# Token sums in the q/k/v stage, gate rows in the last merge phase, weights' squares into free buffers, and B's spatial output in SBUF

## The chip, the core and the metric

The kernel runs on one core of one Trainium2 chip. The metric is the device time of one launch in microseconds (us): the kernel before takes 2449.18 us, the median of three runs. Of the core's engines, TensorE (PE in the profile, PEld for its weight loads) does the matmuls and transposes, VectorE (DVE), ScalarE (ACT) and GpSimd (POOL) the elementwise work, and SyncE (SP) issues most of the DMAs; ACT and POOL issue some.

## The reference

One layer of a mixer network for 2048 sample tokens and 128 prompt tokens (2176 in all, 17 tiles of 128), width 1024. The two groups share the weights and differ in the conditioning vector and in the states that they start from.

```python
shift, scale, gate = ada_mod(c, w_ada, b_ada)          # silu(c) @ w_ada + b_ada
xn = rmsnorm(x, ln_g) * (1 + scale) + shift
qkv, beta, dec, z_a, u_b, v_b, z_b, x_c, z_c, gates = split(xn @ w_in)
qkv = silu(conv3(qkv))                                 # q, k, v of 4 heads x 128
o_a = rmsnorm(gated_delta(q, k, v, g, beta) in both directions) * silu(z_a)   # A
o_b = u_b * (w_spatial @ rmsnorm(v_b) + b_spatial) * silu(z_b)                # B, blocks of 128 tokens
o_c = fft2(x_c).real * silu(z_c)                                              # C
merged = sum over n of sigmoid(gates[n]) * (o[n] @ w_branch[n])               # n = A, B, C
y = rmsnorm(x + gate * (merged @ w_out), final_g)
```

The outputs are y for both groups and the prompt's final states of the delta rule. Everything is float32. The kernel multiplies the large matrices in split form: a value is a float16 high part plus a float16 low part, and a product is three matmuls (high x high, high x low, low x high) into one PSUM bank.

## The kernel before

**Order of the stages.** The conditioning sums (shift and scale; the third part, gate, comes later); normalisation and transposes of x into two SBUF tiles, xh and xl (channels on partitions, 2176 tokens), with z_a's projection; q/k/v (12 column tiles of 128, five token blocks each, four of 512 and one of 128); B's v (17 token tiles); the SGU stage, B's u and z (four column tiles, five blocks); branch C with its Fourier transform; six merge phases; the output projection, whose result, gated and normalised, is stored.

**Who sets the order.** The program is written in one order, and a scheduler of the framework then fixes the order of the instructions on each engine, by priorities and a model of times; evictions written under high priority go first. Within an engine the order does not change on the chip. A class Pace (L244) runs one generator beside the main work: each `tick` adds the main work's estimated us, and for every quota (1.2 in q/k/v, 1.6 later) the generator advances by one yield. In q/k/v the generator is decays (L406): for each of 17 tiles, two broadcast loads of log decays from DRAM (gamR), eight DVE operations (L484), a yield, an exponential on ACT (L486), and a store. From the v stage on it is delta (L821): prep for each of 17 tiles (L540: load q, k, v rows, L548, transpose at L549, norms, products with the decays), base_inverse and level for the triangular solves (L598, L639), then scan_dir for the forward and the backward direction, 17 steps each (L739; its matmuls are `b<-sv,R`, `b<-u,skn`, `b<-S,sk` and, in attend, `b<-u,sqk`), and in the backward direction finish (L804) for each tile: sum of both directions, norm, gate, branch A's output to DRAM, and its square sum (L807 to L818).

**q/k/v (L490 to L516).** Each block's product is evicted by ACT into raw (L503); ps_mm has three PSUM banks. After five blocks the three taps of the conv run on DVE (L506 to L508), sigmoids on ACT (L511), products on POOL (L512), and the column tile goes to DRAM.

**v and SGU.** For each token tile the v stage evicts v, norms it, multiplies it by w_spatial, and writes the result vs to DRAM (L888, L889). The SGU stage reads the blocks of vs back into the ring st (L944), and multiplies u onto them (L948). gate_unit (L839) makes silu(z) and the product (L846 to L852). Beside it runs x_sums (L900): sums of quarters of xh, xl for the merge phases, which use a seven-product scheme for 2 x 2 blocks of tokens and channels (S1 to S4 by 80 POOL operations, L917 to L934, a cast on ACT, L912, and a subtraction on DVE, L913, for each of 32 pieces, and a DMA).

**Branch C** shares a ring, us, between the prompt's product yp (L1078) and later products; cf holds its constants.

**Merge.** The phases are (branch, token half): (1,0), (2,0), (1,1), (2,1), (0,1), (0,0), branch 0 being A. A phase has four items (two column tiles each). merge_item (L1162) computes the sigmoid gates from xh and xl in seven products, then the branch's products, and adds to accumulators mrow, which are kept in DRAM between phases. branch_half (L1126) scales and splits the branch's rows to float16 in side steps, one per unit of work. fetch_gate (L977) loads gate weights one item ahead: squares (L1001) for the scale, sums of quarters on POOL (L1011 to L1016), splits (L1008, L1009, L1020), and a write of the split weights for later phases. In phase 0 each item also makes two of eight gate rows (gate_row, L1283): 128 columns of w_ada, 16 DVE operations (ada_sum, L301 to L308) of 128 columns, two matmuls, a store in DRAM. In the last phase each item prepares two column tiles of w_out (out_w, L1322).

Of the kernel before, what the change touches and what calls it, by code (L numbers as in the profile page):

```python
# [110 lines left out]
def hybrid_flow_kernel(ctx: ExitStack, tc: tile.TileContext, x_prompt, x_sample, state_delta, c, c_ctx, ln_g, w_ada,  # L111
# [294 lines left out]
    def decays():  # L406
# [82 lines left out]

    pace.start(decays(), 1.2)  # L490
    for ct in range(12):
        w = getw(1, 2)
        for half in range(1):
            raw = sb(a1p, [P, LP], "raw")
            G.memset(raw[:, 0:1], 0.0)
            G.memset(raw[:, NS + 1:NS + 3], 0.0)
            G.memset(raw[:, LP - 1:LP], 0.0)
            for t0, tn in TBS:
                ps = bank(ps_mm, [P, tn])
                gemm_T(ps, w, 0, xh[:, :, t0:t0 + tn], xl[:, :, t0:t0 + tn])  # L500
                o = t0 + 1 if t0 < NS else t0 + 3
                with tc.high_priority():
                    A.activation(raw[:, o:o + tn], ps, AF.Copy, scale=w.inv)  # L503
# [27 lines left out]
    def chunk_off(t):  # L531
        return t * P if t < 16 else NS + 2
# [7 lines left out]
    def prep(g, ci, t):  # L540
        tok = sb(dq, [P, 2, WB], "tok")
        qr = sb(dq, [P, H, P], "qr")
        ss = sb(dq, [P, 2, H], "ss2", bufs=2)
        for part in range(3):
# [26 lines left out]
        dc = sb(dq, [P, 2, WB], "dc")  # L571
        SY.dma_start(dc, decD[t])
# [283 lines left out]
    vsD = dram("vs", [4, P, NTOK])  # L856
# [12 lines left out]
    vinv = sb(ep, [P, 4], "vinv", bufs=1)  # L869
    for i in range(4):  # L870
        V.tensor_copy(vinv[:, i:i + 1], vw[i].inv)
    for t in range(NCH):
# [6 lines left out]
        vs = sb(bp, [P, 4, P], "vs")  # L879
# [9 lines left out]
        SY.dma_start(vsD[:, :, t * P:(t + 1) * P].rearrange("g p t -> p g t"), vs)  # L889
# [3 lines left out]

    XSLOT = {"A11": (0, 0), "A12": (0, 1), "A22": (1, 1), "S1": (2, 0), "S2": (2, 1), "S3": (3, 0), "S4": (3, 1)}
    xqD = [{n_: dram(f"xq{h}{n_}", [P, 2, 4, 512], F16) for n_ in XSLOT} for h in range(2)]

    def quarter(t, b, kh):
        return t[:, 4 * kh:4 * kh + 4, 512 * b:512 * b + 512]

    def x_sums(sp):  # L900
        for hf in range(2):
            for n_, b, kh in (("A11", 0, 0), ("A12", 0, 1), ("A22", 1, 1)):
                for l, t in enumerate((xh, xl)):
                    SY.dma_start(xqD[hf][n_][:, l], quarter(t, 2 * hf + b, kh))
            yield 1
            for k in range(4):
                (a11, a12), (a21, a22) = [[[t[:, k + 4 * kh, 512 * b:512 * b + 512] for t in (xh, xl)] for kh in range(2)]
                                          for b in (2 * hf, 2 * hf + 1)]

                def put(n_, v):  # L910
                    o = sb(sp, [P, 2, 512], "xo", F16, bufs=3)
                    A.copy(o[:, 0, :], v)  # L912
                    V.tensor_tensor(o[:, 1, :], v, o[:, 0, :], ALU.subtract)  # L913
                    SY.dma_start(xqD[hf][n_][:, :, k, :], o)

                s1, s2, s3, tm = [sb(sp, [P, 512], n_) for n_ in ("s1", "s2", "s3", "tm")]
                G.tensor_tensor(s1, a21[0], a22[0], ALU.add)  # L917
                G.tensor_tensor(tm, a21[1], a22[1], ALU.add)
                G.tensor_tensor(s1, s1, tm, ALU.add)
                put("S1", s1)  # L920
                yield 1
                G.tensor_tensor(s2, s1, a11[0], ALU.subtract)
                G.tensor_tensor(s2, s2, a11[1], ALU.subtract)
                put("S2", s2)
                yield 1
                tm = sb(sp, [P, 512], "tm")
                G.tensor_tensor(s3, a11[0], a21[0], ALU.subtract)
                G.tensor_tensor(tm, a11[1], a21[1], ALU.subtract)
                G.tensor_tensor(s3, s3, tm, ALU.add)
                put("S3", s3)  # L930
                yield 1
                s4 = sb(sp, [P, 512], "s3")
                G.tensor_tensor(s4, a12[0], s2, ALU.subtract)
                G.tensor_tensor(s4, s4, a12[1], ALU.add)  # L934
                put("S4", s4)
                yield 1

    sps = ExitStack()
    xsums = x_sums(pool(sps, "sp", 1))
    for g in range(4):  # L940
        uw, zw = getw(2, 2)
        for ti, (t0, tn) in enumerate(TBS):
            st = sb(ep, [P, tn], "st", bufs=3)
            SY.dma_start(st, vsD[g][:, t0:t0 + tn])  # L944
# [5 lines left out]
            next(xsums, 0)  # L950
            gate_unit(1, g, ti, zw, st)
            next(xsums, 0)
    for _ in xsums:
        pass
    sps.close()
# [21 lines left out]
    def fetch_gate(i):  # L977
# [22 lines left out]
        for c in range(2):  # L1000
            A.activation(tiles[2 + c][:, :, 1], sts[c], AF.Square, accum_out=ss[:, c:c + 1])  # L1001
# [11 lines left out]
        split(tiles[2], sts[0])  # L1013
        split(tiles[0], tq)
        G.tensor_tensor(tq[:, 0], b21, tq[:, 0], ALU.subtract)
        G.tensor_tensor(tq[:, 1], b22, b12, ALU.subtract)  # L1016
        A.activation(tiles[3][:, 0, 0], b22, AF.Copy, scale=s)
# [3 lines left out]
        split(tiles[1], tq)  # L1021
        for z, t in enumerate(tiles):
            m = 1024 if z == 3 else 2048
            SY.dma_start(gwD[n][j][:, z, 0:m], flat(t)[:, 0:m])
# [30 lines left out]
    for g in range(4):  # L1055
        xw, zw = getw(2, 2)
        for gh in range(1):
            yT = sb(fp, [P, NTOK], "yT", bufs=1)
            Y1 = sb(fp, [P, 64, 32], "Y1")
            for q in range(0, NCH, 4):  # L1060
# [13 lines left out]
                else:  # L1074
                    ps = bank(ps_x, [P, 2 * P])
                    mm(ps, xc[:, 0, :], K["dftcs"])
                    yp = sb(fp, [P, 2 * P], "us", bufs=2)
                    V.tensor_copy(yp, ps)  # L1078
                    ps = bank(ps_x, [P, P])
                    mm(ps, K["dftcs"][:, 0:P], yp[:, 0:P], True, False)  # L1080
                    mm(ps, K["dftms"], yp[:, P:2 * P], False, True)
                    A.copy(yT[:, NS:NTOK], ps)
                pace.tick(1.5 * qn)
            yv = yT[:, 0:NS].rearrange("p (r k) -> p k r", k=64)
            for q4 in range(4):
# [14 lines left out]
                pace.tick(3.5)  # L1100
                us = sb(fp, [P, 8, 32], "us", bufs=2)
# [24 lines left out]
    def branch_half(n, hf, prompt):  # L1126
# [8 lines left out]
        def steps():  # L1135
            for b in range(2):
                for g in range(4):
                    st = sb(big, [P, 512], "mrow", bufs=6)
                    t0 = 1024 * hf + 512 * b
                    SY.dma_start(st, obD[n][g, :, t0:t0 + 512])  # L1140
# [21 lines left out]
    def merge_item(i, o16, side, swap, first):  # L1162
# [5 lines left out]

        def unit():
            pace.tick(2.8)  # L1170
            next(side, 0)

        mr = {}
        for r_, c in ((0, 0), (1, 1), (0, 1), (1, 0)):
            mr[r_, c] = sb(big, [P, 512], "mrow", bufs=6)
            if not first:
                t0 = 1024 * hf + 512 * r_
                SY.dma_start(mr[r_, c], mD[2 * j + c][:, t0:t0 + 512])
# [104 lines left out]
    def gate_row(blk):  # L1283
        st = sb(wp, [P, KT, P], "wst", bufs=2)
        SY.dma_start(st, w_ada_[:, 2 * D + blk * P:2 * D + (blk + 1) * P].rearrange("(k p) c -> p k c", p=P))
        ps = bank(ps_x, [2, P])
        acc = sb(ep, [P, 512], "st", bufs=3)[:, 0:2 * P].rearrange("p (g c) -> p g c", g=2)
        ada_sum(acc, st, range(KT))
        for g in range(2):
            mm(ps, sel[:, g, :], acc[:, g, :], g == 0, g == 1)  # L1290
        gr = sb(big, [2, P], "gr", bufs=1)
        br2 = sb(big, [2, P], "br2", bufs=1)
        SY.dma_start(br2, b_ada_[None, 2 * D + blk * P:2 * D + (blk + 1) * P].to_broadcast([2, P]))
        V.tensor_add(gr, ps, br2)
        SY.dma_start(gateD[:, blk * P:(blk + 1) * P], gr)

    def run_phase(p, each=None):
        n, hf = PH[p]
        o16, inv, side = branch_half(n, hf, PH[p] in FRESH)
        for j in range(4):  # L1300
# [3 lines left out]
            if each is not None:  # L1304
                each(2 * j)
                each(2 * j + 1)
# [3 lines left out]
    run_phase(0, gate_row)  # L1310
    for p in range(1, 4):
        run_phase(p)
# [47 lines left out]

    order = [16] + list(range(8, 16)) + list(range(8))
    run_phase(4)
    run_phase(5, out_w)
# [71 lines left out]
```

## Time and profile before

| | us |
|---|---|
| median of 3 runs | 2449.18 |
| lowest, highest | 2446.91, 2450.38 |
| profiled execution | 2451.27 |
| its span | 2449.5 |

A line of a table by windows gives the stretch in us from the span's start, its length, then for each engine its busy time and number of instructions, then PEclk, the mean clock granted to TensorE (1 is full), the share of time in which DMA engines were busy, and GB/s. A line of the waits gives the waiting engine, its operation and line, what it waited for, and then us in total, the number of times, and the longest. A line of the groups gives line, engine, operation, result and operands with shapes and count, then busy us and mean ns of one, then idle time in front of them with what ended it. A letter q behind an engine marks its queue.

### The profile page before, as it was taken

The page shows a single profiled execution, that of the slowest core. Times are in us where ns is not written, and L with a number is a line of the kernel's source. Part 1 is how long each engine was busy: PE and PEld are TensorE (multiplying, and loading weights), DVE is VectorE, ACT ScalarE, POOL GpSimd, SP SyncE. Part 2 cuts the span into 40 slices and gives each one's busy share as a digit, 9 for nine tenths or more (in the row PEclk, how much of TensorE's full clock was granted, in tenths as well). Part 3 has the DMA queues.
Part 4 walks back from the last instruction along what each step waited for, and adds up shares of the span by engine and source line. Part 5 has one row for each costly group of instructions (what it writes and reads, how often), then busy time and mean ns, then how long its engine had stood idle before and what let it go on. Part 6 is the DMA issues. An engine that isn't in the chain of part 4 may idle for free. (4 is left out here: it accounts for less than half of the span.)

```text
span 2449.5 us, 43951 instructions
## 1 busy us (share of the span) xinstructions
PE 2250.5 (92%) x16804; PEld 1374.8 (56%) x16804; DVE 1439.1 (59%) x3228; ACT 825.3 (34%) x1539; POOL 1026.2 (42%) x1216
## 2 busy tenths in 40 slices
PE   7998999998988898989978879989999999989998
PEld 3564444796444677768555555656665545534443
DVE  5636743467659486655776777766555345452554
ACT  3544533322433333222522224332223233331332
POOL 2411222344986333234553454765443334323453
PEclk9999999998998999999989889999999999989999
DMA  8615622475675756324764556769656556963542
GB/s 287 207 54 191 222 90 77 155 206 125 202 203 150 211 183 155 65 68 144 262 219 152 164 175 206 246 217 327 204 183 217 164 169 218 303 220 118 179 155 103
DMA packets 437436, 440.63 MB, mean 180 GB/s; under 512 B 94449, under 2 KB 333034, under 8 KB 435690
## 3 DMA queue, kind: packets, MB, share of 16 engines
q1 hardware_dynamic: 422282, 384.33, 51.3%
q0 software_dynamic: 10048, 40.13, 4.2%
q10 hardware_dynamic: 4896, 13.37, 1.5%
q8 instruction: 132, 2.16, 0.4%
q14 instruction: 78, 0.64, 0.1%
HBM read 269.35 MB, written 168.39 MB: 179 GB/s over the span
## 5 line engine op out<-in xcount | busy, mean ns | idle before, releaser
L160 PE MATMUL b<-xh,w 128*128 128x512 f16 (+1 forms) x3976 | 1045.3, 350 | 26.4 <-ACT raw L503 13.1
L160 PEld LDWEIGHTS <-w 128*128 128x128 f16 x5964 | 535.1, 99 | 575.6 <-issue 61.1
L160 PE MATMUL b<-xl,w 128*128 128x512 f16 (+1 forms) x1988 | 678.0, 350 | 0.5 <-POOL xl L382 0.4
L160 PE MATMUL b<-big,b 128*128 128x512 f16 (+1 forms) x1440 | 292.9, 355 | 9.9 <-ACT big L1142 3.4
L160 PEld LDWEIGHTS <-b 128*128 128x128 f16 x1440 | 129.7, 99 | 147.3 <-issue 26.3
L160 PE MATMUL b<-w,xh 128*128 128x128 f16 x2176 | 201.0, 224 | 0.0
L160 PE MATMUL b<-w,xl 128*128 128x128 f16 x1088 | 194.9, 224 | 0.0
L160 PEld LDWEIGHTS <-xh 128*128 128x128 f16 x2312 | 181.8, 100 | 4.3 <-issue 3.3
L512 POOL TENSOR_TENSOR cy<-cy,raw 128x545 f32<-128x545 f32 (+1 forms) x48 | 55.5, 1181 | 225.2 <-ACT raw L511 225.2
L756 POOL TENSOR_SCALAR skn<-skn,ed 128x128 f32<-128x128 f32 x136 | 87.9, 661 | 143.7 <-DMA skn<-kv 131.9
L1199 POOL TENSOR_TENSOR mrow<-mrow,sg 128x512 f32<-128x512 f32 x64 | 85.2, 1338 | 146.0 <-DVE sg L1197 104.0
L160 PEld LDWEIGHTS <-xl 128*128 128x128 f16 x1224 | 116.5, 100 | 0.4
L656 POOL TENSOR_TENSOR R<-ec,cst 128x512 f16<-128x512 f16 x68 | 75.2, 1126 | 85.6 <-PE b L160 54.8
L160 PE MATMUL b<-wohi,ml 128*128 128x512 f16 x272 | 103.5, 381 | 1.6 <-DVE ml L1341 1.6
L160 PE MATMUL b<-wohi,mh 128*128 128x512 f16 x272 | 103.8, 382 | 1.2 <-ACT mh L1340 1.2
L160 PE MATMUL b<-wolo,mh 128*128 128x512 f16 x272 | 103.8, 382 | 0.0
L656 POOL TENSOR_TENSOR T<-ec,cst 128x512 f16<-128x512 f16 x68 | 76.2, 1139 | 55.6 <-PE b L160 47.3
L1188 DVE TENSOR_TENSOR sg<-b,st 128x512 f32<-128x512 f32 x69 | 47.3, 688 | 81.8 <-PE b L160 81.6
L160 PEld LDWEIGHTS <-mh 128*128 128x128 f16 x544 | 53.3, 98 | 66.1 <-ACT mh L1340 1.7
L582 POOL COPY nd<-n 32x128 f32<-32x128 f32 x136 | 60.4, 444 | 66.0 <-DVE n L580 60.8
L1182 ACT ACTIVATE sg<-sg,ginv 128x512 f32<-128x512 f32 x69 | 49.5, 718 | 100.2 <-DVE sg L1188 100.2
L382 POOL TENSOR_TENSOR xl<-xm,xh 128x512 f16<-128x512 f32 (+1 forms) x40 | 45.1, 1148 | 58.8 <-ACT xh L381 58.7
(402 smaller groups left out, 3948.6 us busy)
## 6 DMA issues: line engine op xcount, KB each, us to landing
wst<-in_w_in_dram SPq DMA_DIRECT2D x60, 512.0 KB
gw<-w SPq DMA_DIRECT2D x36, 512.0 KB
w<-gw SPq DMA_DIRECT2D x36, 512.0 KB
mrow<-mrg SPq DMA_DIRECT2D x70, 256.0 KB
mrg<-mrow POOLq DMA_DIRECT2D x64, 256.0 KB, 3.7
qkv<-cy POOLq DMA_DIRECT2D x12, 1089.0 KB, 4.4
mrow<-br SPq DMA_DIRECT2D x51, 256.0 KB
dc<-dec SPq DMA_DIRECT2D x17, 512.0 KB
```

What stands on the lines that cost most here:

```text
L160: PE.matmul(out, l, r, start=start, stop=stop, **kw)
L382: G.tensor_tensor(xl[:, k, t0:t0 + tn], t, xh[:, k, t0:t0 + tn], ALU.subtract)
L512: G.tensor_tensor(y[:, c0:c1], y[:, c0:c1], raw[:, 1 + c0:1 + c1], ALU.mult)
L582: G.tensor_copy(nd[32 * B:32 * B + 32, d], h3(n_)[32 * B:32 * B + 32, :, 32 * B:32 * B + 32])
L656: G.tensor_tensor(dst[:, l].rearrange("p h a b c -> p h (a b) c"), wide(ec[:, :, which ^ d, l, :]), bm, ALU.mult)
L756: G.tensor_scalar(kn_[:, hs(h)], kn_[:, hs(h)], ed[:, d, t, h:h + 1], None, ALU.mult)
L1182: A.activation(out, src, AF.Sigmoid, scale=gi)
L1188: V.tensor_tensor(out, ps, u, ALU.add)
L1199: G.tensor_tensor(m, m, sg, ALU.add)
```

## The change

- *Token sums.* x_sums moves from the SGU stage to q/k/v, one step after each block from the third column tile on. It uses the rings sg and st in place of a pool of its own. The write of gamR goes from SP's queue to POOL's.
- *Spatial output.* vs stays in SBUF as one tile (vsS, all 2176 tokens); the 17 writes and 20 reads go, and u is multiplied onto it in place. The pool is closed after the SGU stage.
- *Row loads.* prep issues the loads of dc and of q, k and v rows at its start, followed by one more yield. yp gets a buffer of its own and the second half of the prompt's transform moves behind the first of the four quarters.
- *Weights' squares.* fetch_gate puts the squares, which are only summed, into tiles 0 and 1 in place of 2 and 3; each tile's write is issued as soon as it is made, and the splits are reordered.
- *Merge.* Two side steps per unit; accumulators are allocated and loaded at the third to sixth unit of an item in place of its start; branch rows of phases 2 and 5 (`swapped` is true where the token half has just changed: phases 2 and 5) are loaded on POOL's queue.
- *Gate rows.* Four rows of 256 columns, each from two loads of four channel tiles, between the two out_w of each item of the last phase, in place of eight rows of 128 columns in phase 0.

```diff
-            SY.dma_start(gamR[d], gr)
+            G.dma_start(gamR[d], gr)
...
+    xsums = x_sums()
     pace.start(decays(), 1.2)
...
                 pace.tick(tn / 100)
+                if ct > 1:
+                    next(xsums, 0)
...
     pace.drain()
+    for _ in xsums:
+        pass
...
     def prep(g, ci, t):
         tok = sb(dq, [P, 2, WB], "tok")
-        qr = sb(dq, [P, H, P], "qr")
+        dc = sb(dq, [P, 2, WB], "dc")
+        SY.dma_start(dc, decD[t])
         ss = sb(dq, [P, 2, H], "ss2", bufs=2)
+
+        def load(part):
+            x = sb(dq, [P, H, P], "kq" if part else "qr", bufs=2 if part else 1)
+            SY.dma_start(x, qkvD[part * 4:part * 4 + 4, :, chunk_off(t):chunk_off(t) + P].rearrange("h p t -> p h t"))
+            return x
+
+        rows = [load(part) for part in range(3)]
+        qr = rows[0]
+        yield 1
         for part in range(3):
             ps = bank(ps_d, [P, WB])
-            kq = qr if part == 0 else sb(dq, [P, H, P], "kq", bufs=2)
-            SY.dma_start(kq, qkvD[part * 4:part * 4 + 4, :, chunk_off(t):chunk_off(t) + P].rearrange("h p t -> p h t"))
+            kq = rows[part]
...
-        dc = sb(dq, [P, 2, WB], "dc")
-        SY.dma_start(dc, decD[t])
...
-    vsD = dram("vs", [4, P, NTOK])
+    bv = ExitStack()
+    vsS = sb(pool(bv, "bv", 1), [P, 4, NTOK], "vsS")
...
-        vs = sb(bp, [P, 4, P], "vs")
+        vs = vsS[:, :, t * P:(t + 1) * P]
...
-        SY.dma_start(vsD[:, :, t * P:(t + 1) * P].rearrange("g p t -> p g t"), vs)
...
-            st = sb(ep, [P, tn], "st", bufs=3)
-            SY.dma_start(st, vsD[g][:, t0:t0 + tn])
+            st = vsS[:, g, t0:t0 + tn]
...
-            next(xsums, 0)
             gate_unit(1, g, ti, zw, st)
-            next(xsums, 0)
...
-            A.activation(tiles[2 + c][:, :, 1], sts[c], AF.Square, accum_out=ss[:, c:c + 1])
+            A.activation(tiles[c][:, :, 1], sts[c], AF.Square, accum_out=ss[:, c:c + 1])
...
+        def keep(z):
+            m = 1024 if z == 3 else 2048
+            SY.dma_start(gwD[n][j][:, z, 0:m], flat(tiles[z])[:, 0:m])
...
         def unit():
             pace.tick(2.8)
-            next(side, 0)
...
+            done[0] += 1
+            for _ in range(2):
+                next(side, 0)
+            if 3 <= done[0] < 7:
+                rc = ((0, 0), (1, 1), (0, 1), (1, 0))[done[0] - 3]
+                m = mr[rc] = sb(big, [P, 512], "mrow", bufs=6)
+                if not first:
+                    t0 = 1024 * hf + 512 * rc[0]
+                    SY.dma_start(m, mD[2 * j + rc[1]][:, t0:t0 + 512])
...
     def gate_row(blk):
...
+        cs = slice(2 * D + blk * 256, 2 * D + (blk + 1) * 256)
+        ps = bank(ps_x, [2, 256])
+        for k0 in range(0, KT, 4):
+            st = sb(wp, [P, 4, 256], "wst", bufs=2)
+            SY.dma_start(st, w_ada_[k0 * P:(k0 + 4) * P, cs].rearrange("(k p) c -> p k c", p=P))
+            acc = sb(ep, [P, 512], "st", bufs=3).rearrange("p (g c) -> p g c", g=2)
+            ada_sum(acc, st, range(k0, k0 + 4))
+            for g in range(2):
+                mm(ps, sel[:, g, :], acc[:, g, :], k0 + g == 0, k0 + g == 5)
...
-    run_phase(0, gate_row)
-    for p in range(1, 4):
+    for p in range(4):
         run_phase(p)
...
+    def tail(j):
+        out_w(2 * j)
+        gate_row(j)
+        out_w(2 * j + 1)
+
     order = [16] + list(range(8, 16)) + list(range(8))
     run_phase(4)
-    run_phase(5, out_w)
+    run_phase(5, tail)
```

More of the change, by code (lines that the diff above doesn't have):

```diff
@@ L900, in x_sums @@
[L900 to L936, printed above, removed]
@@ L949, in hybrid_flow_kernel @@
             pace.tick(tn / 100)
-            next(xsums, 0)
             gate_unit(1, g, ti, zw, st)
-            next(xsums, 0)
-    for _ in xsums:
-        pass
-    sps.close()
+    bv.close()
     mD = dram("mrg", [KT, P, NTOK])
@@ L1020, in fetch_gate @@
             V.scalar_tensor_tensor(tiles[3][:, a, 1], b_, s, tiles[3][:, a, 0], ALU.mult, ALU.subtract)
[L1021 to L1024, printed above, removed]
+        keep(3)
     def fetch_branch(i, inv):
@@ L1100, in hybrid_flow_kernel @@
                 pace.tick(3.5)
+                if q4 == 0:
+                    ps = bank(ps_x, [P, P])
+                    mm(ps, K["dftcs"][:, 0:P], yp[:, 0:P], True, False)
+                    mm(ps, K["dftms"], yp[:, P:2 * P], False, True)
+                    A.copy(yT[:, NS:NTOK], ps)
                 us = sb(fp, [P, 8, 32], "us", bufs=2)
@@ L1167, in merge_item @@
         bi = lambda c: binv[:, n * 8 + 2 * j + c:n * 8 + 2 * j + c + 1]
+        mr, done = {}, [0]
         def unit():
             pace.tick(2.8)
-            next(side, 0)
[L1173 to L1178, printed above, removed]
+            done[0] += 1
[7 more added lines that the diff above has]
+                    SY.dma_start(m, mD[2 * j + rc[1]][:, t0:t0 + 512])
         def sig(out, src):
@@ L1283, in gate_row @@
     def gate_row(blk):
[L1284 to L1293, printed above, removed]
+        cs = slice(2 * D + blk * 256, 2 * D + (blk + 1) * 256)
[7 more added lines that the diff above has]
+                mm(ps, sel[:, g, :], acc[:, g, :], k0 + g == 0, k0 + g == 5)
+        gr = sb(big, [2, 256], "gr", bufs=1)
+        br2 = sb(big, [2, 256], "br2", bufs=1)
+        SY.dma_start(br2, b_ada_[None, cs].to_broadcast([2, 256]))
         V.tensor_add(gr, ps, br2)
-        SY.dma_start(gateD[:, blk * P:(blk + 1) * P], gr)
+        SY.dma_start(gateD[:, blk * 256:(blk + 1) * 256], gr)
     def run_phase(p, each=None):
         n, hf = PH[p]
-        o16, inv, side = branch_half(n, hf, PH[p] in FRESH)
+        o16, inv, side = branch_half(n, hf, PH[p] in FRESH, p > 0 and PH[p - 1][1] != hf)
         for j in range(4):
```

68 lines of the change are left out of this document (51 added, 17 removed).

## The prediction

> **What bounds the kernel now.** I read the page first, then the table of windows with one row per stage, then the waits of PE stage by stage, then the groups by line, and beside them the order of instructions in the two built programs. The profiled execution took 2451.27 us, 2.1 us above the median of the three runs (2449.18 us); the sum is made against it.
>
> ```profile
> span 2449.5 us, 43951 instructions
> PE 2250.5 (92%) x16804; PEld 1374.8 (56%) x16804; DVE 1439.1 (59%) x3228; ACT 825.3 (34%) x1539; POOL 1026.2 (42%) x1216
> PE 27%; DMA 4%; DVE 1%; ACT 1%; issue 1%; POOL 1%; SPq 0%; DVEq 0%; POOLq 0%; ACTq 0%
> ```
>
> TensorE is the bound: it is busy 92%, no other engine over 59%. The change leaves the matmuls almost as they are, so all it can win is in the 199 us in which PE stands still and in the time that it runs at half clock. Where those lie, the windows tell.
>
> ```profile
> core 0: us, PE busy (x) PEld busy (x) DVE busy (x) ACT busy (x) POOL busy (x), PEclk, DMA share, GB/s
> 159.00:447.00 288.00, 274.94 (x1729) 137.13 (x1726) 144.31 (x277) 123.75 (x179) 58.49 (x85) 0.98 0.38 131
> 447.00:597.00 150.00, 136.23 (x1949) 131.26 (x1946) 105.11 (x277) 40.63 (x80) 53.09 (x106) 0.95 0.57 163
> 597.00:838.00 241.00, 208.31 (x1153) 109.87 (x1154) 157.47 (x291) 85.28 (x158) 175.41 (x199) 0.93 0.66 192
> 838.00:1190.00 352.00, 318.11 (x3323) 262.24 (x3321) 221.48 (x535) 109.77 (x245) 130.79 (x180) 0.95 0.50 143
> 1255.00:1480.00 225.00, 182.28 (x1555) 124.82 (x1556) 155.78 (x428) 61.57 (x137) 106.82 (x105) 0.89 0.55 174
> 1480.00:1945.00 465.00, 442.58 (x3374) 272.26 (x3373) 284.35 (x629) 145.08 (x312) 233.60 (x258) 0.98 0.71 225
> 1945.00:2141.00 196.00, 193.78 (x1124) 96.69 (x1123) 97.51 (x201) 70.63 (x110) 69.62 (x70) 1.00 0.67 220
> 2141.00:2264.00 123.00, 113.91 (x505) 49.89 (x504) 48.36 (x99) 35.98 (x57) 32.46 (x35) 0.93 0.53 171
> ```
>
> These are, in order: q/k/v, B's v stage, the SGU (u and z of B), Fourier branch C, merge phase 0, phases 1 to 3, phase 4, phase 5. For each I take what is lost as idle time of PE plus (1 - PEclk) times the length: q/k/v 13.1 + 5.8 = 19 us, v 21, SGU 32.7 + 16.9 = 50, C 33.9 + 17.6 = 51, phase 0 42.7 + 24.8 = 67, phases 1 to 3 22.4 + 9.3 = 32, phase 4 2, phase 5 18. Per us of stage, phase 0 is worst (0.30) and the SGU next (0.21); phases 1 to 3, with the same merge work and scan steps of the same kind beside it, lose 0.07.
>
> The clock belongs in the account, since it falls behind a stall:
>
> ```profile
> 703.00:705.00 2.00, 0.61 (x5) 0.58 (x6) 1.36 (x3) 1.88 (x5) 2.00 (x3) 1.00 0.23 69
> 705.00:708.50 3.50, 3.50 (x11) 1.19 (x9) 3.50 (x7) 1.14 (x4) 3.46 (x4) 0.51 0.42 150
> ```
>
> After 1.4 us of idle in two, PE has the half clock for the next 3.5 us and loses 1.7 us more. So I price a stall that goes at its idle time and about half again. [...]
>
> **The change part by part.**
>
> *Gate rows out of phase 0, and the scan there (-45).*
>
> ```profile
> PE b L160 <- DVE T L699: 11.7, 6, 4.7
> PE b L160 <- ACT Q L707: 6.6, 4, 3.9
> PE b L160 <- DVE Q L708: 5.2, 4, 2.6
> 1255.00:1300.00 45.00, 29.62 (x246) 22.13 (x247) 37.47 (x107) 13.51 (x31) 24.14 (x23) 0.81 0.65 202
> L308 DVE SCALAR_TENSOR_TENSOR st<-wst,scT,st 128x128 f32<-128x128 f32 x84 | 26.3, 374 | 0.1
> 1300.06 0.59 PE L160 MATMUL b<-xh,w 128*128 128x512 f16 x2
> 1300.71 0.59 PE L160 MATMUL b<-xh,w 128*128 128x512 f16 x2
> ```
>
> The waits and the L308 row are of the window of phase 0. PE waits there for the links of the delta rule's chain (T, Q), and DVE, which makes most links, is busy 37.5 of 45 us in its worst piece; 26.3 us of the stage's DVE time is the gate rows. Three matmuls start in 0.65 us (the timeline's rows), 0.22 us each. With that price I count the other PE work that stands, in program order, between one scan step and the next. Before, seven of the 16 intervals in the first direction have under 6 us of it, two of them none, so PE must wait out the chain. In the changed order intervals 6 to 16 all have 13 us or more, and only 2 to 5 have 6 to 9. At the rate of phases 1 to 3 (0.07) phase 0 would lose 15 us and not 67: -52. I take -45, for the short intervals that remain. Bounds: -23, the three idle rows alone, and -60, a loss of 7.
>
> *Start of phase 4 (+12).* The work is not gone but taken from elsewhere. Before, the scan ends (in PE's program order) some 70 us of PE work ahead of the first branch-A matmul of phase 4; after, its last transposes stand directly in front of it. A wait comes up where there were 2 us of loss.
>
> ```profile
> PE b L815 <- DVE o L812: 8.2, 4, 3.4
> L807 POOL TENSOR_TENSOR o<-o,of 128x512 f32<-128x512 f32 x17 | 21.6, 1268 | 42.3 <-DVE o L729 38.4 <-DVE bsc L176 3.9
> L812 DVE TENSOR_TENSOR o<-o,oss 128x512 f32<-128x512 f32 x17 | 20.3, 1194 | 12.9 <-POOL oss L164 12.8
> L817 DVE SCALAR_TENSOR_TENSOR o<-b,pc,of 128x512 f32<-128x512 f32 x17 | 12.7, 747 | 9.3 <-PE b L815 9.3
> ```
>
> Phase 4's scale needs the squares of all tiles. The last tile's chain is L807 (1.3 us), a square, a sum, the root, L812 (1.2), transposes, L817 (0.7), a square, the scale's links and the scaled copy: ten operations, at about 0.9 us each 9 us, with a third more for the clock +12. Bounds: +3 (one wait as the longest at L815, 3.4 us) and +20 (each link is held 0.7 us more by an eviction in work).
>
> *B's spatial output in SBUF, token sums out of the SGU (-15, and -1 in the v stage).*
>
> ```profile
> PE b L549 <- DMA qr<-qkv: 6.4, 5, 2.6
> PE b L160 <- DVE sg L848: 5.3, 1, 5.3
> PE b L160 <- DVE st L948: 3.7, 1, 3.7
> L948 DVE SCALAR_TENSOR_TENSOR st<-b,winv,st 128x512 f32<-128x512 f32 (+1 forms) x20 | 13.3, 665 | 24.9 <-DMA st<-vs 24.9
> L912 ACT CAST xo<-s 128x512 f16<-128x512 f32 x32 | 19.1, 614 | 31.7 <-POOL s L923 12.1 <-POOL s L934 8.0 <-POOL s L929 5.7
> L913 DVE TENSOR_TENSOR xo<-s,xo 128x512 f16<-128x512 f32 x32 | 34.7, 1096 | 15.8 <-ACT xo L912 15.6
> L918 POOL TENSOR_TENSOR tm<-xl 128x512 f32<-128x512 f16 x8 | 10.5, 1317 | 0.4
> ```
>
> The first three rows are PE's waits in the SGU. The 20 reads of vs go, and with them DVE's idle 24.9 us. The token sums take 32 casts (19.1 us of ACT), 32 subtractions (34.7 us of DVE) and 80 POOL operations (1.3 us by the L918 row: some 104 us) out of a stage where POOL is busy 175 of 241 us and the gate unit's own POOL products must come in between. At the v stage's rate (21 in 150, 0.14) the SGU would lose 34 and not 50: I take -15, with the first row's data waits in it. Bounds: 0, since a DVE that reads sooner may just wait for PE (DVE is the second engine that the delta chain needs here), and -34, at q/k/v's rate (0.066). The v stage's 17 writes go as well, so SP comes to the delta rows behind them sooner (-3 of the stage's 21; 0 to -10), and the load of the DFT constants now waits for the SGU's last POOL product, with some 10 us of PE work between it and the first use (+2; 0 to +8).
>
> *Rows of q, k, v loaded one yield ahead; yp in its own buffer (-12).*
>
> ```profile
> PE b L160 <- DVE us L1078: 6.2, 2, 5.0
> PE b L549 <- DMA qr<-qkv: 3.3, 3, 2.3
> ```
>
> These are PE's waits in stage C. The first is the copy that shares its ring with us, and moves behind q4 = 0; the second is the row load at the head of each tile. Together 9.5 us idle and, with half of a 3.5 us half-clock stretch for each of the two long ones, 12. The extra yield puts delta's end later, which is in the phase 4 term. Bounds: 0 (another link is late next: L1068's copy of xc feeds the same matmuls) and -16.
>
> *Token sums in q/k/v (+12).*
>
> ```profile
> PE b L160 <- ACT raw L503: 13.1, 6, 4.9
> ACT XB L486 <- DVE XB L484: 22.7, 7, 8.6
> ACT dc L486 <- DVE dc L484: 16.5, 5, 7.9
> ```
>
> All of this stage's PE waits are for the eviction L503 on ACT, which stands behind exponentials that wait up to 8.6 us for DVE, who waits for the row of log decays. The sums bring ACT from 124 to 143 us of 288, DVE from 144 to 179, POOL from 58 to 162; on SP the first nine writes of sums stand ahead of the loads of log decays, later ones between them; and each cast waits, in ACT's order, for two or three POOL operations (2.6 to 3.9 us). A unit of 512 tokens takes PE 275/60 = 4.6 us and it has three banks, so a hold of under 9 us is covered. I take two or three stalls as long as the longest (4.9 us), +12, between -5 (later log decays come one at a time and wait less) and +40 (eight such stalls), nearer to nothing since the cover exceeds a cast's wait.
>
> *Gate rows in phase 5 (+8).* The four rows are now of 256 columns, 64 operations:
>
> ```profile
> L308 DVE SCALAR_TENSOR_TENSOR aacc<-ast,scT,aacc 128x256 f32<-128x256 f32 x24 | 9.9, 475 | 0.0
> ```
>
> 64 x 0.475 = 30 us of DVE, from 48 to 79 of 123 us. Evictions go first on DVE, but one in work holds them 0.5 us, and the loads share a ring with w_out's. I take 8 operations in a row (3.8 us) as one wait of 2 us behind half of them, twice in the phase with its clock (6 us), and 2 us for the gate's last store, which the output stage reads back. Bounds: 0 (all lies beside PE) and +25 (each of the eight half rows costs 3 us).
>
> *The weights' squares* go into a buffer that is free: ACT's row for them waited 4.3 us for PE in all, not on the path; 0, to -2. *Two side steps per unit and accumulators loaded later*, and branch rows on POOL's queue for phases 2 and 5: 0 (-3 to +5).
>
> Sum: -45 + 12 - 15 - 1 - 12 + 12 + 8 = -41, so 2451.3 - 41 = 2410 us.
>
> **The rivals.**
>
> (a) *Faster still, 2370.* If phase 0 falls to phases 1 to 3's rate (-52), SGU to q/k/v's (-34), and phase 4 and q/k/v cost 5 each: -52 - 34 - 12 + 5 + 5 + 8 - 1 = -81. For it: the changed order has no empty step. Against: DVE's own chain stays.
>
> (b) *The SGU doesn't gain, and phase 4 costs its upper bound: 2410 + 15 + 8 = 2433.* For it: the longest waits there, sg 5.3 us, come from ACT and DVE, not from vs. I call it the smaller gain.
>
> (c) *The scan is bound by its own chain, no change: 2450.* A step's links are in series; if more PE work between them doesn't hide them, the phase 0 term is -5 and not -45, and the sum -1. Against: in phases 1 to 3 the same links are hidden behind 17 to 20 us of work.
>
> (d) *Slower: q/k/v's evictions stand in ACT's queue, 2498.* Place: between L503's evictions, 32 casts wait for POOL. Price of one that holds PE: 4.9 us and half of a 6.8 us half-clock stretch, 8.3. With 12 of 32 it is 100 instead of 12: 2498. It decides the sign from six stalls (50 us) on. For it: the exponentials alone held ACT up to 8.6 us, and PE up to 4.9. Against: 9 us of cover.
>
> (e) *DVE and POOL shut each other out in q/k/v, 2470.*
>
> ```profile
> L198 DVE SCALAR_TENSOR_TENSOR w<-wst,wsc,w 128x1024 f16<-128x1024 f32 x36 | 47.6, 1333 | 3.1 <-ACT w L197 3.1
> L1009 DVE SCALAR_TENSOR_TENSOR w<-wst,wsc,w 128x1024 f16<-128x1024 f32 x12 | 19.6, 1634 | 2.3 <-ACT w L1008 2.1
> ```
>
> One form takes 1.33 us in one place and 1.63 where POOL makes sums of the same weights: a stretch of a fifth. Were it exclusion, the first half of q/k/v would need 72 + 35 us of DVE (half of its row, and L913) and 29 + 104 of POOL, 240 us in 144; half of the 96 us over would reach PE through the exponentials, 48, and a quarter of that in clock: +60 on the forecast. Against: in the SGU 157 us of DVE and 175 of POOL go into 241. [...]
>
> **How the numbers follow.** Forecast 0.42, (a) 0.17, (b) 0.16, (c) 0.10, (d) 0.08, (e) 0.07. A measurement of this kernel tells about 0.2% (4.9 us) from no change. Faster: 0.42 + 0.17 + 0.16 and a little of (c): 0.77. Same: 0.06, most of (c). Slower: (d), (e) and the rest of (c), 0.17. The range leaves out (d), (e) and the ends of (a) and (c): 2365 (a, and 5 for its spread) to 2455 (c, and 5 for its own spread). The median is taken at the profiled run's value; the 2 us between them are within the step of 5.
>
> **What would show it.** Right: in phase 0 PE idle falls from 43 to under 20 us and PEclk rises above 0.95; DMA waits of L549 and st<-vs are gone; a wait of about 8 us for big at the start of phase 4; ACT raw waits below 25 us in q/k/v. Wrong, to the slower side: ACT raw waits over 50 us, or a scan that still waits for T and Q; to the faster side: a loss of phases 0 to 3 at 0.05 throughout and no wait at phase 4.

## The result, and the profile after

The changed kernel takes 2411.39 us (median of 4 runs, 2402.30 to 2417.11), the kernel before 2448.05 beside it (4 runs, 2445.70 to 2450.38): a ratio of 0.985, 95% interval 0.981 to 0.988. The forecast was 2410. The sum came out, but three of its terms (phase 0, the SGU, q/k/v) lie outside their own bounds, and the errors cancelled: that the sum fits so well is in part luck.

The profiled execution of the changed kernel is its fastest (2402.30 us, span 2400.5), 9 us below the median, so its trace has to account for some 49 us where the medians differ by 37. In the windows of after, in the columns known from before, the stages are q/k/v, the SGU, C, phase 0, phases 1 to 3, phase 4, phase 5:

```profile
158.00:492.00 334.00, 285.02 (x1721) 139.43 (x1719) 221.10 (x306) 139.63 (x211) 166.16 (x164) 0.92 0.41 138
637.00:859.00 222.00, 208.44 (x1254) 116.92 (x1253) 125.38 (x300) 73.37 (x136) 89.71 (x146) 0.98 0.66 182
859.00:1212.00 353.00, 320.91 (x3437) 264.40 (x3435) 227.57 (x570) 113.32 (x256) 136.05 (x182) 0.96 0.49 139
1212.00:1420.00 208.00, 205.52 (x1745) 132.32 (x1744) 146.20 (x363) 84.50 (x169) 92.05 (x90) 1.00 0.65 211
1420.00:1930.00 510.00, 493.88 (x3742) 299.29 (x3740) 312.42 (x671) 154.63 (x333) 276.90 (x307) 0.99 0.70 223
1930.00:2100.00 170.00, 148.07 (x877) 73.97 (x876) 92.72 (x200) 62.59 (x99) 62.06 (x63) 0.94 0.71 234
2100.00:2218.00 118.00, 112.91 (x515) 49.09 (x514) 66.00 (x146) 30.53 (x48) 32.47 (x34) 0.99 0.53 175
```

q/k/v, which holds the same main work in both kernels, grew from 288 to 334 us: PE is idle 49 us in place of 13, and the clock fell from 0.98 to 0.92. Phase 0 is all but full: 2.5 us idle at clock 1.00. Phase 4 is now idle for 22 us, at a clock of 0.94.

Stage lengths can't be compared further, as the delta rule's work moves between stages. So I use from here on the **loss** of a stage: its length less the time that its matmuls take from start to start at full clock (the median of each form in the same trace). A stage runs from its own first eviction to the next stage's: phase 0, for instance, from its first gate sigmoid to that of phase 1. Loss in us, worked out from each profiled execution:

| | q/k/v | v | SGU | C | ph. 0 | ph. 1 | ph. 2, 3 | ph. 4 | ph. 5 | all stages |
|---|---|---|---|---|---|---|---|---|---|---|
| before | 20 | 11 | 56 | 58 | 84 | 32 | 11 | 2 | 16 | 315 |
| after | 65 | 15 | 20 | 56 | 9 | 26 | 10 | 30 | 10 | 264 |
| gate_only | 19 | 10 | 54 | 56 | 6 | 27 | 12 | 37 | 9 | 256 |
| prep_only | 21 | 14 | 46 | 56 | 84 | 32 | 7 | 4 | 16 | 306 |
| sums_only | 65 | 11 | 33 | 48 | 92 | 24 | 3 | 3 | 17 | 319 |
| gate_back | 65 | 15 | 20 | 56 | 94 | 29 | 3 | 3 | 4 | 315 |
| gate_light | 17 | 10 | 54 | 60 | 68 | 29 | 10 | 2 | 16 | 293 |
| gate_acc | 19 | 13 | 57 | 54 | 46 | 31 | 13 | 14 | 15 | 285 |
| cast_pool | 52 | 13 | 20 | 54 | 11 | 26 | 8 | 29 | 11 | 247 |
| late_sums | 65 | 19 | 20 | 60 | 9 | 30 | 10 | 31 | 11 | 281 |
| sums_v | 16 | 51 | 36 | 52 | 15 | 20 | 13 | 42 | 8 | 278 |
| sums_v_q100 | 16 | 53 | 65 | 40 | 14 | 37 | 5 | 12 | 10 | 275 |
| gate_prep | 19 | 12 | 46 | 54 | 6 | 24 | 14 | 32 | 12 | 244 |
| gate_prep_q100 | 16 | 15 | 66 | 44 | 8 | 24 | 15 | 7 | 11 | 232 |

(The last column has the first stage and the output stage too, 22 to 27 us in all kernels.) PE's waits of after in the whole span, with the time in all, the number and the longest, begin with

```profile
PE b L160 <- ACT raw L551: 44.8, 8, 15.8
PE b L874 <- DVE o L871: 8.9, 3, 5.2
PE b L160 <- DVE sg L907: 8.7, 2, 7.0
PE b L610 <- DMA qr<-qkv: 8.4, 3, 6.0
```

The eviction of q/k/v (L503 before, L551 now) costs PE 44.8 us where it cost 13.1, in 8 waits of which the longest is 15.8. The waits for T and Q in phase 0, 23.5 us before, are not in this list; in phase 0 the largest is 2.0. The loads of rows still cost 8.4 us (10.2 before), now in few waits.

### The profile page after: what moved, and what is told of

Read it like the earlier page. It is cut to its first block, busy times and chain, and to the rows that moved or that the text cites. A ratio compares the mean times of both kernels' runs of the same rounds, so it can differ in the third digit from the quotient of the medians.

```text
span 2400.5 us, 43732 instructions
## 1 busy us (share of the span) xinstructions
PE 2224.7 (93%) x16804; PEld 1356.3 (56%) x16804; DVE 1466.3 (61%) x3160; ACT 824.1 (34%) x1539; POOL 1044.2 (43%) x1234
## 4 chain that ended last, share of the span: by engine, by line
PE 47%; DVE 11%; DMA 11%; SPq 3%; POOL 2%; issue 2%; ACT 2%; DVEq 0%; POOLq 0%; ACTq 0%
PE b L160 46%; DMA wst<-in_w_in_dram 2%; DMA wst<-in_w_ada_dram 2%; DVE E L679 2%; DVE Et L678 2%; SPq L692 1%; SPq L670 1%; DMA Et<-nd 1%; DVE st L308 1%; DMA wst<-in_w_branch_dram 1%; DMA qr<-qkv 1%; PE b L610 1%; DMA mrow<-mrg 1%; DMA mrg<-mrow 1%; DVE w L1016 1%
## 5 line engine op out<-in xcount | busy, mean ns | idle before, releaser
L160 PE MATMUL b<-xh,w 128*128 128x512 f16 (+1 forms) x3976 | 1047.8, 351 | 57.4 <-ACT raw L551 44.8
L171 DVE CAST wscb<-wss 128x1 bf16<-128x1 f32 x69 | 10.6, 153 | 102.9 <-ACT w L195 62.9
```

Source lines behind the costliest of these rows:

```text
L160: PE.matmul(out, l, r, start=start, stop=stop, **kw)
```

## The experiments

Theory T: the gate rows alone make phase 0's loss. Theory R: it was prep's extra yield. For q/k/v, theory E: the sums on POOL hold DVE; theory D: the sums' casts hold ACT.

**gate_only: the kernel before, with only the gate rows moved.**

```diff
-    run_phase(0, gate_row)
-    for p in range(1, 4):
+    for p in range(4):
         run_phase(p)
...
-    run_phase(5, out_w)
+    run_phase(5, tail)
```

(gate_row and tail as in the change.)

> The kernel before, with only the gate rows moved (four of 256 columns, last phase). Theory T: the rows alone cause phase 0's loss, and with them gone the first direction's intervals have 13 to 20 us of other PE work from the sixth on (as in the built order here). Loss of phase 0 (idle plus excess over full clock, first gate sigmoid of phase 0 to that of phase 1) falls from 84 to under 25 us; the scan's end moves into phase 4, which then loses 20 to 30 in place of 3; net -45, so 2403, and 2395 to 2415. Rival R: the gain came from the extra yield of prep and the row loads; then phase 0 still loses over 60 us and the time is 2440 or more.

2398.15 us (2393.29 to 2403.02), ratio 0.978, 0.975 to 0.981. Phase 0's loss falls from 84 to 6 us, phase 4's rises from 2 to 37, phase 5's falls from 16 to 9. T holds, R doesn't. One part of the change, alone, gains at least as much as all of it (a ratio of 0.978 against 0.985, and 0.980 in the second sample of the changed kernel, late_sums below).

**prep_only: the kernel before, with only prep changed** (loads at its start, one more yield).

> The kernel before, with only prep changed (dc, q, k, v rows loaded at its start, one more yield); yp stays on its ring. T: the row waits in the SGU and C go (10 us), phase 0's loss stays over 60 us, since its intervals without other PE work stay in the order; 2436 to 2446. R: phase 0's loss falls under 40 us, time under 2420.

2433.24 us (2431.14 to 2439.68), ratio 0.993, 0.990 to 0.995. Phase 0 still loses 84 us; the SGU gains 10. T again. The median is 3 us beyond the faster end of what was expected.

**sums_only: the kernel before, with only x_sums moved to q/k/v.**

> The kernel before, with only the token sums moved to q/k/v (and gamR's write on POOL's queue). If the SGU's gain of 37 us (loss 56 to 19) is that of the sums, the SGU's loss is under 30 here, though vs is still read from DRAM; q/k/v loses about 65 in place of 19 us; the net is +15 (2450 to 2475). Rival: the gain is that of vs in SBUF; then the SGU still loses over 45 and the time is 2485 or more.

2459.24 us (2455.87 to 2466.30), ratio 1.0045, 1.003 to 1.006: by itself, this part makes the kernel slower. q/k/v loses 45 us more, as in the full change. The SGU's loss falls from 56 to 33, just missing the "under 30", though vs is still read from DRAM: 23 of the SGU's 36 us are the sums'. With prep_only's 10, some 3 us are left for B's spatial output in SBUF, if the parts add up; no run has that edit alone.

**gate_back: the changed kernel with the gate rows as before.**

> The changed kernel with the gate rows back as they were (eight of 128 columns in phase 0). T: phase 0's loss is back above 60 us, phase 4's falls under 10; net +35 to +50 on the changed kernel, so 2445 to 2460, the same as before. R: phase 0 stays under 30 us, the time within 10 us of the changed kernel's 2411.

2451.79 us (2449.28 to 2456.80), ratio 1.001, 0.999 to 1.003. Phase 0 loses 94 us, phase 4 3. Without the move of the gate rows the change as a whole gains nothing.

**gate_light and gate_acc: why do the gate rows cost phase 0 so much?** gate_light leaves out seven of eight products of each row and group (the gate is then that of the first 128 channels of the condition); gate_acc keeps all 128 and gives their sums a buffer of their own.

```diff
-        ada_sum(acc, st, range(KT))
+        ada_sum(acc, st, range(1))
```

```diff
-        acc = sb(ep, [P, 512], "st", bufs=3)[:, 0:2 * P].rearrange("p (g c) -> p g c", g=2)
+        acc = sb(big, [P, 2 * P], "gacc", bufs=1).rearrange("p (g c) -> p g c", g=2)
```

> The kernel before, with seven of the eight products of each gate row and group left out: 16 DVE operations in all in place of 128, so the gate is that of the first 128 channels of the condition only. Rows, loads, rings and places stay. Theory V (DVE's load is what phase 0 suffers from): phase 0's loss falls from 84 to under 40 us, the time to 2405 to 2420. Theory O (order: rows that hold a buffer of the ring st until their load has come keep the merge's own products back, and the order has intervals without other PE work): those intervals are still in the built order, so phase 0 loses 65 or more and the time is 2435 to 2450.

> The kernel before, all 128 operations of the gate rows in phase 0, but their sums in a buffer of their own and no longer in the ring st. The built order has no interval without other PE work from the sixth on but two of 3.5 and 7 us. Theory V: phase 0 still loses 70 or more, 2440 to 2450. Theory O: its loss falls under 45 us, the scan ends later and phase 4 loses 20 to 30; 2405 to 2425.

gate_light 2426.78 us (2424.27 to 2436.72), ratio 0.990, 0.986 to 0.993; gate_acc 2418.53 (2418.13 to 2423.06), ratio 0.986, 0.983 to 0.989. Taking away 112 DVE operations leaves 68 of phase 0's 84 us; taking away the shared buffer leaves 46, and of the intervals without other PE work most are gone. The windows of phase 0 in gate_light and then in gate_acc:

```profile
1194.00:1484.00 290.00, 251.25 (x2174) 169.75 (x2174) 181.79 (x467) 94.59 (x203) 129.44 (x135) 0.92 0.62 196
```

```profile
1196.00:1451.00 255.00, 230.75 (x1901) 145.21 (x1902) 191.65 (x504) 79.54 (x171) 109.51 (x109) 0.97 0.61 192
```

DVE is freer in gate_light (182 us of 290) than in gate_acc (192 of 255), and PE idles more (39 us against 24). So O, taken away alone, is worth more than V (38 us against 16): rows hold one of three buffers of st while the merge's products wait for one. The expectations were met in part. gate_light's loss is where O has it (65 or more), its time between the ranges of V and O. gate_acc's time is in O's range, its loss just misses "under 45", and phase 4 loses 14 in place of 20 to 30. The rest, from 46 down to 6, goes only with the move of the rows; whether the loads' ring wst or DVE holds it stays open, and so V's full share does.

**cast_pool: the changed kernel with the sums' casts on POOL.**

```diff
-                    A.copy(o[:, 0, :], v)
+                    G.tensor_copy(o[:, 0, :], v)
```

> The changed kernel with the token sums' 32 casts on POOL, so that no cast stands in ACT's order in front of an eviction. Theory D (casts that wait for POOL hold ACT): the eviction's wait in q/k/v falls from 45 to under 20 us, the stage from 335 to about 300, the time to 2375 to 2390. Theory E (POOL's sums hold DVE's operations with two SBUF operands, so the exponentials are late): with 32 operations more on POOL the wait stays above 35 us and the stage at 330 to 350; 2405 to 2425.

2390.39 us (2383.66 to 2394.28); beside it the kernel before at 2453.62, ratio 0.974, 0.970 to 0.977. The stage falls from 334 to 320 us and the eviction's wait from 44.8 to 39.4. The wait is as E has it, the stage is between the two, and the time is at the end of D's range. D has a share, about 14 us of 46; the rest is not the casts. Against late_sums, whose order is the changed kernel's and which ran beside it, this is 15 us better.

**late_sums: sums from the seventh column tile on.**

```diff
-                if ct > 1:
+                if ct > 5:
```

> The changed kernel with the token sums from the seventh column tile on in place of the third, when most rows of log decays are through; all operations and their engines stay. E: the mean of a decay operation (L484) falls from 745 to under 500 ns, the eviction's wait from 45 to under 20 us, the stage to 295 to 310; 2375 to 2395. D: the casts stand in ACT's order as before, so six or more stalls remain, the stage at 320 or more; 2400 to 2415.

2405.53 us (2400.68 to 2417.83), ratio 0.980, 0.976 to 0.983. It tells nothing: the scheduler put the sums where they had been (the first starts at 154 us, the last at 334, as in the changed kernel, at 153 and 334), since nothing in the program holds them back. It serves as a second sample of the changed kernel, and shows how far two sets of runs differ (0.980 here, 0.985 above).

**sums_v: the sums in B's v stage.** Here they did move: the first starts at 463 us, the last at 642.

```diff
-                if ct > 1:
-                    next(xsums, 0)
...
         pace.tick(5.2)                # in the loop over token tiles of v
+        for _ in range(2):
+            next(xsums, 0)
```

> The changed kernel with the token sums in B's v stage (two steps after each token tile) in place of q/k/v; the same operations on the same engines. E: with no sums beside them the decay operations (L484) are back at 420 to 450 ns in the mean, the eviction's wait in q/k/v at 10 to 20 us, the stage at 288; in the v stage the norms' operations with two SBUF operands are stretched instead, 5 to 20 us there; 2370 to 2390. If the eviction's wait comes from anything else in the change (the write of gamR on POOL's queue, say), it stays over 35 us and the time is over 2400.

2412.86 us (2411.45 to 2415.13), ratio 0.983, 0.981 to 0.986. q/k/v is back at 285 us, its eviction's wait at 11.2 us, and L484 at a mean of 400 and 439 ns:

```profile
159.00:444.00 285.00, 273.85 (x1741) 137.38 (x1740) 143.91 (x275) 123.73 (x180) 61.93 (x87) 0.98 0.39 133
PE b L160 <- ACT raw L550: 11.2, 3, 5.0
```

So the whole loss of q/k/v came from the sums, and none from gamR's write on another queue, which is still in. But the loss moved, and the time is no better than the change's: v loses 51 us in place of 15, more than the 5 to 20 expected, and the SGU 36 in place of 20. In v the norm's product on DVE (L943 in after, L939 here), 514 ns at most in the changed kernel, takes up to 1490:

```profile
L943 DVE TENSOR_SCALAR sg<-sg,vss x17: 475/485/514, 520.8 to 629.8; 128x512 f32<-128x512 f32 x17
```

```profile
L939 DVE TENSOR_SCALAR sg<-sg,vss x17: 473/487/1490, 474.9 to 638.2; 128x512 f32<-128x512 f32 x17
```

The sums also share the ring sg with it, and the two causes weren't separated.

**sums_v_q100: the same, with delta's quota at 1.0.**

```diff
-QUOTA = 1.6
+QUOTA = 1.0
```

> The same with the quota of the pace at 1.0 in place of 1.6, so that delta's steps come sooner. In the built order the scan now ends 79 us of PE work ahead of phase 4's first branch product (before: 70; changed kernel: 0). If phase 4's loss is the wait for the scan's end, it falls from 30 to under 8 us; the stages v and SGU carry more delta work per us and may lose 5 to 15 more; 2355 to 2380. If the loss comes from phase 4's own weights, it stays above 20.

2399.90 us (2391.99 to 2413.28), ratio 0.977, 0.974 to 0.981, slower than expected. Phase 4's loss falls from 42 to 12 us, not to the "under 8". What goes is the wait for the scan's end: nothing is lost any more in the first of the phase's four items (25 in sums_v). The 12 us that are left are all in its last item and have another cause (see phase 5 below). The SGU gives 29 back, twice what was expected at most.

**gate_prep: before, with the gate rows moved and prep changed; gate_prep_q100: the same with quota 1.0.**

> The kernel before, with the gate rows moved and prep changed, the token sums, vs, yp, squares and merge left as before. Were the parts additive (-50 and -15), 2383; the sums and the other edits of the change are then a net loss of some 28 us against this kernel. Range 2375 to 2395.

> The kernel before with the gate rows moved, prep changed, and the quota at 1.0. In the built order the scan ends 35 us of PE work ahead of phase 4's first branch product (0 at quota 1.6). Where the end of the scan is what phase 4 waits for, its loss falls from 32 us to 10 or less; the SGU, which carries more of delta's prep, gives back 10 to 20 of that, as it did with the sums in the v stage: 2365 to 2385. If that is given back in full, the time stays at 2384.

gate_prep 2384.47 us (2380.74 to 2392.82), ratio 0.972, 0.969 to 0.975: the two parts add up, and the rest of the change is a net loss of some 18 to 31 us (0.972 against the changed kernel's 0.980 and 0.985). gate_prep_q100 2368.93 (2364.13 to 2371.34), ratio 0.969, 0.966 to 0.971 (the kernel before took 2445.40 beside it): phase 4 loses 7 in place of 32 us, the SGU 66 in place of 46. It beats both kernels by the edits of two small parts and one number. Its page:

```profile
span 2367.4 us, 43838 instructions
PE 2215.9 (94%) x16804; PEld 1358.1 (57%) x16804; DVE 1438.1 (61%) x3160; ACT 824.0 (35%) x1539; POOL 1021.4 (43%) x1216
```

## Why the prediction was right, and where its terms were not

**Phase 0: -45 forecast, -75 measured.** The mechanism was right and the term too small: the loss went from 84 to 9 (67 by the prediction's window, which began some 60 us later). My caution, "for the short intervals that remain", was not needed. That DVE is busy with the rows, which the step gives beside the empty intervals, was worth the less of the two when taken away alone (16 us against 38).

**Phase 4: +12 forecast, +28 measured, of which +16 are this step's.** By the four items of the phase, the changed kernel loses 18 us in the first, nothing in the second and third, and 12 in the last; the kernel before loses 2 in the first and nothing in the others. The loss of the first item is the one that was forecast, and its mechanism was right: in sums_v_q100 and gate_prep_q100, where the scan ends earlier, it is 0 and 3 us (25 in sums_v and in gate_prep, at quota 1.6). The step priced one chain of ten links; in the trace, PE waits in this item seven times, 12.0 us in all, for the branch rows' scale, branch weights, gate weights and their scales in turn. The last item's 12 us are the gate rows' (see phase 5). Together phases 0 to 4 come to -54 (from 129 to 75 lost), -65 without that item, where -33 was forecast.

**q/k/v: +12 forecast, +46 measured; the step failed at "nearer to nothing since the cover exceeds a cast's wait".** It priced ACT's queue by the casts, which are a third of it, and laid aside the rival that decided, (e). The decay operations of before and of after, with minimum, median and maximum in ns:

```profile
L484 DVE SCALAR_TENSOR_TENSOR XB<-XB,tok,cst x72: 337/344/1237, 187.1 to 308.5; 128x128 f32<-128x128 f32 x72
```

```profile
L484 DVE SCALAR_TENSOR_TENSOR XB<-XB,tok,cst x72: 335/346/1424, 206.6 to 361.5; 128x128 f32<-128x128 f32 x72
L484 DVE SCALAR_TENSOR_TENSOR dc<-dc,tok,cst x64: 335/342/1766, 209.5 to 349.2; 128x128 f32<-128x128 f32 x64
```

Sorted by whether a tensor-tensor operation of POOL ran at the same time: of the 136, 88 ran alone in 335 to 351 ns, and 48 beside POOL, with a median of 1235 ns, which is about one POOL sum (1.2 us). In before 19 of 136 met POOL (median 1230 ns). The row was there to be read: its mean of 418 hid two values, 344 and 1237. The worst case of after, in order of start, first on DVE and then on POOL:

```profile
299.41 6.81 DVE L556 TENSOR_SCALAR cy<-raw,pc 128x2178 f32<-128x2178 f32 x1 [1.41 <-ACT raw L551]
```

```profile
299.35 1.16 POOL L522 TENSOR_TENSOR sg<-sg,xl 128x512 f32<-128x512 f32 x1
300.47 1.26 POOL L528 TENSOR_TENSOR sg<-sg,sg 128x512 f32<-128x512 f32 x1
301.69 1.16 POOL L532 TENSOR_TENSOR sg<-xh,sg 128x512 f32<-128x512 f16 x1
302.81 1.14 POOL L515 TENSOR_TENSOR sg<-xh 128x512 f32<-128x512 f16 x1
303.92 1.14 POOL L533 TENSOR_TENSOR sg<-sg,xl 128x512 f32<-128x512 f32 x1
```

An operation of 1.36 us (the median of the 12 of L556) takes 6.81: five POOL operations run in a row meanwhile (to 305.1 us), and it ends 1.2 us behind the last. The path to PE runs through ACT (the timeline of DVE, then that of ACT):

```profile
286.73 7.65 DVE L484 SCALAR_TENSOR_TENSOR XB<-XB,tok,cst 128x128 f32<-128x128 f32 x8
```

```profile
287.96 0.62 ACT L509 CAST st<-sg 128x512 f16<-128x512 f32 x1 [3.07 <-POOL sg L517]
288.59 1.28 ACT L486 ACT_TABLE_LOAD   x1
294.41 1.06 ACT L486 ACTIVATE XB<-XB 128x1024 f32<-128x1024 f32 x1 [4.54 <-DVE XB L484]
...
296.42 0.67 ACT L551 ACTIVATE raw<-b,winv 128x512 f32<-128x512 f32 x1
```

Eight decay operations take 7.65 us where eight of 344 ns would take 2.8; the exponential waits for them, the eviction stands behind the exponential (in the trace of after, ACT's 1298 operations, DVE's 3160 and POOL's 1092 all ran in the built order), and PE's three banks run out: its wait of 15.8 us ends at 297.1 us. Of these, ACT stood idle 4.5 us for the decays and 3.1 for a sum of POOL, whose cast is next in its order; the rest is ACT's own work and a wait for the conv. The other waits divide in the same way: four more (7.3, 6.0, 4.5 and 1.1 us) come behind an exponential for which ACT had idled 3.8 to 7.6 us, and two (3.2 and 6.6) behind a cast that had waited 8.0 us for POOL; the eighth is 0.3 us. With the 3.1 us, the waits behind casts come near the 14 us that cast_pool gives to them. So (e) gave the larger part of the cause and (d) the smaller, both by ACT's queue, at a price between my +12 and (e)'s +60. The stage's busy time on DVE says the same: the prediction added up 179 us, and it is 221. The evidence that I set against (e), sums of busy time of both engines in a stage, can't refute it: the 6.81 us above count as busy in whole, for an operation that takes 1.36 alone. And not every operation is stretched: of the same form as the decays but with one operand in PSUM, `sv<-b,neg,sv` (L821 in after) takes 339 to 353 ns in the 37 cases beside a tensor-tensor operation of POOL and 335 to 352 in the 91 without.

**SGU: -15 forecast, -36 measured.** Mechanism right, size off: sums 23, prep 10, vs about 3. The evidence that I led with, DVE's 24.9 us of idle time before the reads of vs, was the part worth least: idle time of an engine that isn't the bound. The v stage, where -1 was forecast, lost 4 us more; why was not followed.

**Row loads and yp in C: -12 forecast, -2 measured.** The wait for us is gone, but C has one of 4.1 us for the DFT constants (the prediction had put 2 there), one of 7.0 for the gate unit's product on DVE (L907), and one of 6.0 for qr is in the SGU. The term's lower bound, that another link is late next, was the likelier. prep's gain of 15 us is elsewhere, mostly in the SGU.

**Phase 5: +8 forecast, -6 in the table, +5 with the last item of phase 4.** The scheduler put the first gate row into that item, and there the rows cost PE its longest wait of phases 4 and 5:

```profile
PE b L160 <- DVE st L1249: 7.7, 1, 7.7
```

```profile
2090.18 0.61 DVE L306 TENSOR_SCALAR st<-wst,scT 128x256 f32<-128x256 f32 x2 [7.57 <-DMA wst<-in_w_ada_dram]
2090.71 0.48 DVE L308 SCALAR_TENSOR_TENSOR st<-wst,scT,st 128x256 f32<-128x256 f32 x1
2091.11 0.68 DVE L1249 TENSOR_TENSOR st<-b,st 128x512 f32<-128x512 f32 x1
```

DVE stands idle until the load of the row has come (issued at 2077.8 us), and the merge's own addition (L1249) stands behind the row's products. So the size was near, but not the reason: the step priced DVE's operations, and PE waited for a load in front of them. The 30 us of DVE lie beside PE, as the lower bound had it. The last item of phase 4 and phase 5 together lose 16 us in the kernel before, 21 in the changed one, 7 in gate_back and 14 in gate_only; why they lose less without the rows (7) than before (16) was not followed.

The rivals: (a) is half true (phase 0 did even better than -52, the SGU -36), and q/k/v ate what it won. (b), (c) are out, (e) is true in the larger part of the cause and (d) in the smaller.

Of the signs named beforehand, phase 0's idle time and clock came (2.5 us, 1.00) and the wait for vs is gone. The waits for rows are not (8.4 us), phase 4 starts with seven waits in place of one, and the eviction's wait in q/k/v is 44.8 us, not below 25.

## What to carry to other kernels

A forecast by stages can be right in sum with three terms off by 20 to 35 us in both directions, so ask the trace for each term, and try the parts singly: here two of the parts alone, with a quicker pace, are some 27 to 39 us better than the whole (0.969 against 0.980 and 0.985). Moving work to an engine that looks idle is not free: here the decays on DVE, on the way to the bound, took 1235 ns in place of 341 where they met POOL's operations. Look at minimum and maximum of a group, not at its mean. When stages are compared, look where in a stage its loss lies: part of phase 4's belonged to work of phase 5. And when a scheduler fixes the order, count how much of the bound's work stands between the links of a serial chain, and look which shared buffers took it away.

## What was not expected of the hardware

The decay operation of DVE (L484, two SBUF operands), 341 ns alone (median of 88), took 1235 ns (median of 48) beside POOL operations of 1.2 us; a tensor-scalar operation of 2178 columns (L556), 1356 ns alone (median of 10), took 6807 ns while five of them ran in a row. One sum of POOL took 1763 ns in the mean (L526, 8 of them: median 1204, longest 5259) in q/k/v, and 1211 in the SGU stage of before (L927, 8 of them: median 1157, longest 1479).
